# Three pairs of chunks as block products in the later FFNs, and weight splits of 2048 columns

## The chip, the cores and the metric

The kernel runs on one core of one Trainium2 chip. The metric is the device time of one execution in microseconds. The engines in the text are TensorE (PE, with its weight loads as PEld), VectorE (DVE), ScalarE (ACT), GpSimd (POOL) and SyncE (SP, which issues nearly all of the DMAs here).

## The reference

A streaming-encoder trunk of two layers on 256 tokens of width 1024, in float32. Each layer has three sub-layers, each between two RMS norms: an FFN, a mixer (differential attention beside an mLSTM), and a second FFN.

```python
def _swiglu(h, w_in, w_out):
    gate, up = jnp.split(h @ w_in, 2, axis=-1)
    return (jax.nn.silu(gate) * up) @ w_out
...
    for l in range(DEPTH):
        g = norm_gains[l]
        h = _swiglu(_rmsnorm(x, g[0]), ffn_w_in[l, 0], ffn_w_out[l, 0])
        x = x + 0.5 * _rmsnorm(h, g[1])
        lam_init = 0.8 - 0.6 * math.exp(-0.3 * l)
        h = _mixer(_rmsnorm(x, g[2]), mix_w_in[l], mix_w_out[l], da_lambda[l], da_subln_g[l],
                   lam_init, ml_conv_w[l], ml_conv_b[l], ml_gate_b[l], ml_norm_g[l])
        x = x + _rmsnorm(h, g[3])
        h = _swiglu(_rmsnorm(x, g[4]), ffn_w_in[l, 1], ffn_w_out[l, 1])
        x = x + 0.5 * _rmsnorm(h, g[5])
```

The hidden width of an FFN is 2816. w_in is 1024 x 5632 (gate and up), w_out 2816 x 1024.

## The kernel before

**Phases and chunks.** The six sub-layers are phases 0 to 5; phases 0, 2, 3 and 5 are FFNs. An FFN is cut into 11 chunks of 256 hidden columns. Tokens are two tiles of 128, t = 0 and 1. A chunk's in part multiplies the tokens with 512 columns of w_in (256 gate, 256 up). Its weights come as two pieces of 128 x 2048 floats, one for each half of the 1024 rows (kh = 0, 1). Its out part multiplies the hidden values with one piece of w_out and adds to four PSUM banks (bk), which collect over all of the chunks.

**Products in three matmuls.** Each float operand is split in a high part of reduced precision and the rest. A product is then three matmuls of 128 x 128 by 128 x 512: high by high, high by low, low by high (`mm3`, L506 to L508). A plain chunk's in part is 2 tokens x 8 row blocks x 3 = 48 matmuls, an out part 24.

**Splitting weights.** `fetch` (L288) loads a piece into a raw buffer (tag wr, three of them; every fourth piece goes to wx). `halved` (L295, L296) makes the high part with a cast on ScalarE and the low part with a subtraction on VectorE, 1024 columns at a time. The halves live in seven buffers each for wl and wh, and, for three halves out of ten, in two of the six k4 buffers: five pieces in all. In the mixer k4 holds that phase's own tiles (gt, conv, two qkT, vd), and no weights are put there. `self.turns` puts the first splits of a phase behind named operations of the norms around the phase's start.

**Pairs.** `pair(c)` does the in parts of chunks c and c+1 as one product of 2 x 2 blocks (token tiles by chunk columns) with seven block products P1 to P7 in place of eight (Strassen's scheme in Winograd's form). Each block product is 12 matmuls (L762). For it, `pair_blocks` makes four sums of weight pieces on VectorE (L322) and splits seven pieces in place of four: P1 is b11, P5 the sum b11 + b12, P6 that plus b22, P7 is b12 + b22, P2 is b21, P3 is b22, P4 the running sum plus b21. The running sum lies in two buffers, qk and wt (`spare`), which also hold the mixer's data, and in phases 2, 3 and 5 the normalised tokens of the phase. `pair_tokens` makes four sums of token blocks from these (L357 to L368, split at L676 and L677), in three steps S0, S1, S2. The results are put together by seven VectorE operations (u, v, h0; L780 to L799) and two silu.

**From hidden values to the out part.** The hidden values of a chunk must be turned before they can be multiplied with w_out: ScalarE sorts bytes into planes (L648), a DMA transposes (L650), ScalarE puts them together as hT (L656), then hh and hl are split off (L676, L677). There are four buffers each of hh and hl.

**Stationary weights.** The last chunk, 10, is done with the weights as the stationary operand (`in_turned`, L737 and L742), which gives the hidden values already turned, so that no DMA is needed. It wants each token's norm factor as a row (`token_scales`, L684) and its own evacuation (`ffn_block`, L695 to L700).

**Order.** `STEPS` is the order of an FFN after chunks 0 and 1: I is a plain chunk, P a pair, L the load of an out piece, O an out part, S a step of the token sums.

```python
STEPS = "I2 L1 S0 O0 I3 L2 S1 O1 S2 P4 L3 O2 L4 O3 I6 L5 O4 I7 L6 O5 P8 L7 O6 L8 O7 I10 L9".split()
END = (8, 9, 10)
```

The order of the instructions on each engine is set when the program is built, by the framework's planner: an instruction that stands earlier in the program (or under `high_priority`) goes first among those that the planner has as ready, and later ones pass it while it isn't. Buffers are given from the free ones in the same way. `after` adds an edge for the order alone. From "ending" to "running" TensorE follows program order: there the out parts of chunks 8 to 10 are done, first for token 0, then for token 1, with the norms and the next phase's first chunk between.

## Time and profile before

| | |
|---|---|
| median of 3 runs | 940.39 us (940.22 to 941.68) |
| the profiled execution | 940.3 us |
| its span, first to last instruction | 938.5 us |
| mean granted TensorE clock | 0.998 |
| HBM read | 177.01 MB, 190 GB/s over the span |

The page has the busy share of each engine; views by stage, by group and in order of time are behind it. The bounds of the phases are read from the transposes of the norms (L532): FFN 0 to 180, mixer to 288, FFN to 467, FFN to 643, mixer to 751, FFN to the end. In the views a name like `wl<-wr,wh` is the written tile and the read ones, `x12` is a count, `[0.80 <-PE ptr L532]` is idle time ahead of an instruction and what ended it. Matmuls are pipelined: one of 512 columns is listed with some 0.39 us, and the next starts 0.23 us after it.

### The profile page before, as it was taken

The page shows a single profiled execution, that of the slowest core. Times are in us where ns is not written, and L with a number is a line of the kernel's source. Part 1 is how long each engine was busy: PE and PEld are TensorE (multiplying, and loading weights), DVE is VectorE, ACT ScalarE, POOL GpSimd, SP SyncE. Part 2 cuts the span into 40 slices and gives each one's busy share as a digit, 9 for nine tenths or more (in the row PEclk, how much of TensorE's full clock was granted, in tenths as well). Part 3 has the DMA queues.
Part 4 walks back from the last instruction along what each step waited for, and adds up shares of the span by engine and source line. Part 5 has one row for each costly group of instructions (what it writes and reads, how often), then busy time and mean ns, then how long its engine had stood idle before and what let it go on. Part 6 is the DMA issues. An engine that isn't in the chain of part 4 may idle for free.

```text
span 938.5 us, 12082 instructions
## 1 busy us (share of the span) xinstructions
PE 931.4 (99%) x4427; PEld 771.5 (82%) x4427; DVE 775.5 (83%) x1079; ACT 668.4 (71%) x1033; POOL 29.4 (3%) x57
## 2 busy tenths in 40 slices
PE   9999999999999999999999999999999999999997
PEld 7888888888888888888888888888888888888885
DVE  7989797889867899788698987968898588986974
ACT  8967786677856868676587865866778478766862
POOL 2000000000020000000000000000001100000000
PEclk9999999999999999999999999999999999999999
DMA  9957857346362866838468585473554348486531
GB/s 354 342 169 275 251 192 218 119 152 221 138 232 90 303 167 225 303 107 309 121 237 257 172 267 189 155 237 135 189 193 169 146 157 302 148 300 184 186 115 46
DMA packets 69882, 189.34 MB, mean 202 GB/s; under 512 B 45274, under 2 KB 46426, under 8 KB 49086
## 3 DMA queue, kind: packets, MB, share of 16 engines
q1 hardware_dynamic: 69246, 187.95, 59.1%
q8 instruction: 35, 0.57, 0.2%
q10 hardware_dynamic: 576, 0.61, 0.2%
q14 instruction: 25, 0.20, 0.1%
HBM read 177.01 MB, written 1.05 MB: 190 GB/s over the span
## 4 chain that ended last, share of the span: by engine, by line
PE 99%; DVE 0%; ACT 0%; POOLq 0%; DVEq 0%; issue 0%; ACTq 0%
PE pin L506 11%; PE pin L508 10%; PE pin L507 10%; PE bk L506 10%; PE bk L507 10%; PE bk L508 10%; PE ptr L762 9%; PE pin L762 7%; PE ptr L507 3%; PE ptr L506 3%; PE ptr L508 3%; PE ptr L737 2%; PE pin L737 2%; PE ptr L532 1%; PE ptr L1100 1%; PE pin L742 1%
## 5 line engine op out<-in xcount | busy, mean ns | idle before, releaser
L296 DVE TENSOR_TENSOR wl<-wr,wh 128x1024 fp32r<-128x1024 f32 x262 | 313.6, 1221 | 42.2 <-ACT wh L295 39.4
L295 ACT ACTIVATE wh<-wr 128x1024 fp32r<-128x1024 f32 x262 | 269.5, 1055 | 55.9 <-PE bk L508 15.8
L506 PE MATMUL pin<-wh,both 128*128 128x512 f32 x432 | 171.3, 399 | 0.0
L507 PE MATMUL pin<-wl,both 128*128 128x512 f32 x432 | 168.4, 390 | 0.0
L508 PE MATMUL pin<-wh,both 128*128 128x512 f32 x432 | 168.2, 390 | 0.0
L507 PE MATMUL bk<-wl,hh 128*128 128x512 f32 x352 | 136.3, 389 | 0.0
L506 PE MATMUL bk<-wh,hh 128*128 128x512 f32 x352 | 135.8, 390 | 0.0
L508 PE MATMUL bk<-wh,hl 128*128 128x512 f32 x352 | 133.4, 389 | 0.0
L508 PEld LDWEIGHTS pin<-wh,both 128*128 128x128 f32 x432 | 81.1, 188 | 17.4
L506 PEld LDWEIGHTS pin<-wh,both 128*128 128x128 f32 x432 | 81.3, 188 | 17.2 <-issue 0.7
L507 PEld LDWEIGHTS pin<-wl,both 128*128 128x128 f32 x432 | 81.3, 188 | 15.5
L295 ACT ACTIVATE wh<-wx 128x1024 fp32r<-128x1024 f32 x62 | 64.3, 1055 | 31.9 <-PE bk L508 10.2
L762 PE MATMUL ptr<-wh,both 128*128 128x512 f32 x256 | 84.0, 389 | 0.0
L296 DVE TENSOR_TENSOR wl<-wx,wh 128x1024 fp32r<-128x1024 f32 x62 | 74.7, 1220 | 10.2 <-ACT wh L295 9.5
L508 PEld LDWEIGHTS bk<-wh,hl 128*128 128x128 f32 x352 | 66.1, 188 | 13.8
L506 PEld LDWEIGHTS bk<-wh,hh 128*128 128x128 f32 x352 | 66.1, 188 | 13.5
L507 PEld LDWEIGHTS bk<-wl,hh 128*128 128x128 f32 x352 | 66.1, 188 | 13.4
L762 PE MATMUL pin<-wh,both 128*128 128x512 f32 x192 | 63.0, 389 | 0.0
L762 PEld LDWEIGHTS ptr<-wh,both 128*128 128x128 f32 x256 | 48.0, 188 | 10.0
L507 PE MATMUL ptr<-wl,both 128*128 128x512 f32 x128 | 49.8, 389 | 0.0
L508 PE MATMUL ptr<-wh,both 128*128 128x512 f32 x128 | 49.8, 389 | 0.0
L762 PE MATMUL ptr<-wl,both 128*128 128x512 f32 x128 | 49.8, 389 | 0.0
(263 smaller groups left out, 1464.2 us busy)
## 6 DMA issues: line engine op xcount, KB each, us to landing
wr<-in_w_dram SPq DMA_DIRECT2D x131, 1024.0 KB, 5.1
wx<-in_w_dram SPq DMA_DIRECT2D x31, 1024.0 KB, 5.0
gpost<-in_gpost_dram SPq DMA_DIRECT2D x6, 512.0 KB, 6.2
wr<-in_w_dram SPq DMA_DIRECT2D x2, 512.0 KB, 6.3
wr<-in_w_dram SPq DMA_DIRECT2D x3, 256.0 KB, 4.5
x<-in_x_dram SPq DMA_DIRECT2D x3, 256.0 KB, 5.2
h<-planes SPq DMA_TRANSPOSE x32, 3.3
out_dram<-x SPq DMA_DIRECT2D x2, 256.0 KB, 2.1
```

The lines of the kernel that those rows point to most:

```text
L295: ia = nc.scalar.activation(hi, raw, AF.Copy)
L296: iv = nc.vector.tensor_tensor(lo, raw, hi.bitcast(F32), op=ALU.subtract)
L506: mm(ps, xh, wh, start=start, stop=False)
L507: mm(ps, xh, wl, start=False, stop=False)
L508: mm(ps, xl, wh, start=False, stop=stop)
L532: nc.tensor.transpose(ptr[:, k, :], x[:, (4 * hf + k) * P:(4 * hf + k + 1) * P], self.ident)
L737: self.nc.tensor.matmul(b, self.cols(w[kh], k)[0][:, c], both[kh][:, k].rearrange("p i t -> p (i t)"), start=kh == 0 and k == 0, stop=Fals ...
L742: self.nc.tensor.matmul(b[:, 0:NT * P], self.cols(w[kh], k)[1][:, c], both[kh][:, k, 0:NT].rearrange("p i t -> p (i t)"), start=False, sto ...
L762: self.nc.tensor.matmul(b, st[:, k, :], self.cols(w, k)[mv], start=new and k == n == 0, stop=k == 3 and n == 2, skip_group_check=True)
L1100: self.T(ptr[:, b, :], a[:, b * P:(b + 1) * P], self.tr.ident)
```

## The change

- **Two orders.** Phase 0 has `FIRST_STEPS` with the pairs (4,5) and (9,10) and plain chunks 6, 7 and 8. Phases 2, 3 and 5 have the new `STEPS` with three pairs, (2,3), (6,7) and (9,10), and plain chunks 4, 5 and 8. The token sums S0 to S2 now stand ahead of the pair (2,3) in these.
- **No stationary weights.** `in_turned`, `token_scales`, `ffn_block` and `ffn_turned` are gone. Chunk 10 is the second half of the last pair.
- **Wide splits.** A weight piece is cast and split in one operation of 2048 columns each (`whole`), and so are the block sums. In the mixer, and while `turns` has entries at a phase's start, pieces are split in halves as before.
- **Buffers.** wl and wh become one pool `w` of seven tiles of 2048 columns, and k4 has three such tiles. The mixer's k4 tiles are halves of one (`t4`). The running sum is one tile, `sums`; qk and wt are its halves.
- **Order on TensorE.** P4 of a pair is put behind the last matmul of P3. The second token of the out part of chunk 3 is put behind the pair (6,7), and that of chunk 6 and both of chunk 7 behind the pair (9,10).
- **Small moves.** The load of the post-norm gains and, in phase 0, of the mixer's constants is a step of its own, G0, behind O0. The first weight splits of the next phase are put behind the first token's operands of the last pair instead of those of chunk 10.

```diff
-STEPS = "I2 L1 S0 O0 I3 L2 S1 O1 S2 P4 L3 O2 L4 O3 I6 L5 O4 I7 L6 O5 P8 L7 O6 L8 O7 I10 L9".split()
+FIRST_STEPS = "I2 L1 S0 O0 G0 I3 L2 S1 O1 S2 P4 L3 O2 L4 O3 I6 L5 O4 I7 L6 O5 I8 L7 P9 L8 O6 L9".split()
+STEPS = "S0 S1 S2 P2 L1 O0 G0 I4 L2 O1 L3 O2 I5 L4 O3 P6 L5 O4 L6 O5 I8 L7 P9 L8 O6 L9".split()
...
     def t4(self, nm, shape):
-        return self.k4.tile(list(shape), F32, tag="k4", name=self.name(nm))
+
+        if self.lent is None:
+            pair = self.k4.tile([P, 2, 1024], F32, tag="k4", name=self.name(nm))
+            v, self.lent = pair[:, 0], pair[:, 1]
+        else:
+            v, self.lent = self.lent, None
+        return v[0:shape[0]].rearrange("p (a b) -> p a b", a=shape[1])
...
     def piece(self):
 
 
+        if self.four and not self.turns:
+            return self.whole(self.fetch())
         parts = self.begin_piece()
         return [parts(), parts()]
...
+    def whole(self, raw):
+
+        lo, hi = self.piece_tiles()
+        self.cut = self.nc.scalar.activation(hi, raw, AF.Copy)
+        self.nc.vector.tensor_tensor(lo, raw, hi.bitcast(F32), op=ALU.subtract)
+        return [(hi[:, j], lo[:, j]) for j in range(2)]
...
     def spare(self):
         if self.parts is None:
-            self.qk = self.ded.tile([P, 4, S], F32, name="qk")
-            self.wt = self.ded.tile([P, NT, 2, 2, P], F32, name="wt")
-            self.parts = [self.qk.rearrange("p b s -> p (b s)"), self.wt.rearrange("p t a b j -> p (t a b j)")]
+            self.sums = self.ded.tile([P, 2, 1024], F32, name="sums")
+            self.parts = [self.sums[:, j] for j in range(2)]
+            self.qk = self.parts[0].rearrange("p (b s) -> p b s", b=4)
+            self.wt = self.parts[1].rearrange("p (t a b j) -> p t a b j", t=NT, a=2, b=2)
         return self.parts
...
         def add(out, a, b):
-            for j in range(2):
-                self.nc.vector.tensor_tensor(out[j], a[j], b[j], op=ALU.add)
+            self.nc.vector.tensor_tensor(out, a, b, op=ALU.add)
...
+    def piece_tiles(self):
+
+        v = []
+        for nm in ("wl", "wh"):
+            pool, tag = (self.k4, "k4") if self.lend and self.tiles % 10 in (2, 5, 8) else (self.w, "w")
+            v.append(pool.tile([P, 2, 1024], F32R, tag=tag, name=self.name(nm)))
+            self.tiles += 1
+        return v
...
-        def out_part(c, t, h, wo):
+        def out_part(c, t, h, wo, behind=()):
             for hf in range(2):
                 for k in range(2):
-                    self.mm3(po[t][hf], *h[t][k], *self.cols(wo, 2 * k + hf),
-                             start=c == 0 and k == 0, stop=c == NC_FF - 1 and k == 1)
+                    i = self.mm3(po[t][hf], *h[t][k], *self.cols(wo, 2 * k + hf),
+                                 start=c == 0 and k == 0, stop=c == NC_FF - 1 and k == 1)
+                    self.after(i, behind)
...
-            product(b4, s4, w["P3"], False)
+            i = product(b4, s4, w["P3"], False)
...
-            product(b3, xT[1][1], w["P4"], False)
+            ended[c] = [product(b3, xT[1][1], w["P4"], False, [i])]
...
                 for t in range(NT):
-                    out_part(c, t, hs[c], wo[c])
-        rows = self.token_scales(r)
-        banks = [[self.bank_pin() for _ in range(2)], [self.bank_tr() for _ in range(2)]]
-        in_turned(banks, ws, both)
+                    out_part(c, t, hs[c], wo[c], ended.get(c + 3, []) if t else [])
+        wo[END[-1]] = self.piece()
+        pair_ready([self.cut])
 
         yield "ending"
-        with self.tc.high_priority():
-            hs[END[-1]] = self.ffn_turned(banks, rows)
-        wo[END[-1]] = self.piece()
+        for t in range(NT):
+            out_part(END[0] - 1, t, hs[END[0] - 1], wo[END[0] - 1], ended[END[0] + 1])
...
-        wr, wl, wh, trp, k4 = pool("wr", 3), pool("wl", 7), pool("wh", 7), pool("tr", 4), pool("k4", 6)
+        wr, w, trp, k4 = pool("wr", 3), pool("w", 7), pool("tr", 4), pool("k4", 3)
```

## The prediction

> **What bounds the kernel now.** I read the page's busy shares first, then the busy time by stage, the chain of waits, the groups of instructions by form, and last the order of time around a phase's start and around a pair.

> ```profile
> PE 931.4 (99%) x4427; PEld 771.5 (82%) x4427; DVE 775.5 (83%) x1079; ACT 668.4 (71%) x1033; POOL 29.4 (3%) x57
> ```
> ```profile
> 288.00:467.00 179.00, 179.00 (x815) 149.00 (x814) 149.86 (x184) 127.11 (x171) 2.18 (x4) 1.00 0.63 212
> 467.00:643.00 176.00, 176.00 (x800) 146.37 (x799) 148.24 (x183) 127.71 (x171) 2.32 (x6) 1.00 0.63 209
> ```

> The columns of the second fence are stretch, length, then busy time and count of PE, weight loads, DVE, ACT, POOL, granted clock, DMA share, GB/s. Each stretch is one FFN. TensorE is never idle in them, at full clock, so matmuls taken out are hidden by nothing. VectorE is the next engine: 148 to 150 us, 29 us below the stretch. The chain of waits, in order of time, shows the pitch of matmuls and what lies inside a pair:

> ```profile
> 426.00 1.13 PE pin L762 x5
> 427.13 0.23 PE bk L507
> 427.36 0.45 PE bk L508 x2
> ...
> 430.53 0.91 PE bk L506 x4
> 431.44 2.72 PE ptr L762 x12
> ```

> L762 is a block product: 12 matmuls in 2.72 us, 0.2267 each. The bk rows between are an out part (24 matmuls, 5.44 us): the pair's products leave holes, and out parts fill them. That cover decides this change.

> **What the change removes on TensorE.** A pair does the in part of two chunks in 7 x 12 = 84 matmuls, two plain chunks in 96. Phases 2, 3 and 5 get a third pair: 3 x 12 x 0.2267 = 8.2 us. Phase 0 keeps two pairs, at other chunks: 0. The stage with stationary weights (L737, L742, two transposes) goes in all four FFNs:

> ```profile
> 441.25 1.07 PE L737 MATMUL pin<-both,wh 128*128 128x512 f32 x4
> ```
> ```profile
> 452.63 0.40 PE L506 MATMUL bk<-wh,hh 128*128 128x512 f32 x1
> ```

> It runs from 441.25 to 452.63, 11.38 us, where a plain chunk costs 48 x 0.2267 = 10.88. So 0.50 goes four times, 2.0 us. Together TensorE loses 10.2 us of work. The profiled execution took 940.3 us (its span 938.5 and 1.8 around it, the median of the runs 940.39), so the floor is 930.1.

> **What it adds on VectorE and ScalarE.** The prices of the operations:

> ```profile
> L296 DVE TENSOR_TENSOR wl<-wr,wh 128x1024 fp32r<-128x1024 f32 x262 | 313.6, 1221 | 42.2 <-ACT wh L295 39.4 <-PE bk L508 1.5 <-ACT sil L267 0.8
> L677 DVE TENSOR_TENSOR hl<-hT,hh 128x256 fp32r<-128x256 f32 x80 | 31.2, 419 | 15.6 <-ACT hh L676 15.6
> L322 DVE TENSOR_TENSOR wt<-wt,wr 128x1024 f32<-128x1024 f32 x14 | 17.1, 1219 | 0.0
> L640 DVE SCALAR_TENSOR_TENSOR h<-pin,rs,sil 128x256 f32<-128x256 f32 x30 | 14.2, 478 | 2.6 <-ACT sil L267 2.6
> L697 DVE TENSOR_TENSOR su<-su,rows 128x256 f32<-128x256 f32 x16 | 6.6, 421 | 0.2
> L799 DVE SCALAR_TENSOR_TENSOR v<-v,rs,u 128x512 f32<-128x512 f32 x8 | 6.0, 745 | 0.0
> L784 DVE TENSOR_TENSOR v<-u,ptr 128x512 f32<-128x512 f32 x8 | 5.4, 681 | 0.0
> ```
> ```profile
> L295 ACT ACTIVATE wh<-wr 128x1024 fp32r<-128x1024 f32 x262 | 269.5, 1055 | 55.9 <-PE bk L508 15.8 <-PE ptr L762 12.3 <-PE pin L508 8.3
> L656 ACT ACTIVATE hT<-h 128x1024 uint16<-128x1024 uint16 x32 | 43.7, 1364 | 7.0 <-DMA h<-planes 7.0
> L648 ACT ACTIVATE planes<-h 128x1024 uint16<-128x1024 uint16 x32 | 33.6, 1050 | 17.5 <-DVE h L640 17.5
> L676 ACT ACTIVATE hh<-hT 128x256 fp32r<-128x256 f32 x80 | 29.0, 409 | 0.3
> L267 ACT ACTIVATE sil<-pin,rs 128x256 f32<-128x256 f32 x30 | 14.0, 466 | 16.1 <-PE pin L508 12.2 <-POOL rs L521 3.8
> L676 ACT ACTIVATE both<-aT 128x512 fp32r<-128x512 f32 x16 | 10.0, 624 | 1.8 <-DVE aT L365 1.7
> ```
> ```profile
> 353.86 3.50 DVE L296 TENSOR_TENSOR wl<-wr,wh 128x1024 fp32r<-128x1024 f32 x3
> ```

> No row has 2048 columns. From 512 to 1024 a DVE operation grows by 1.221 - 0.681 = 0.54, so I take 2.29 for 2048. Back to back, operations overlap: three in 3.50 is one each 1.14 us, 0.08 under the duration. So 2048 cost 2.21 where two halves cost 2.28: 0.07 saved a piece (bounds: 0, and 0.15 where neither form overlaps a neighbour). ScalarE: 1.055 + 2 x (1.055 - 0.624) = 1.92.

> [...]

> A third pair brings three more split pieces (3 x 2.21 = 6.6) and four more block sums (8.8). The 33 pieces and 8 sums that grow wide save 41 x 0.07 = 2.9. Evacuations nearly cancel: seven operations of 0.68 to 0.745 come, ten of about 0.42 from the turned stage go. VectorE goes from 149 to about 161.5 us per phase, TensorE from about 176 to 173: 93% instead of 84%. ScalarE gains three splits, 5.8, on 127, and follows. Loads stay at 33 pieces a phase. It fits on average, so each stretch must be looked at.

> **The new first pair, chunks 2 and 3.** Now it comes straight after chunks 0 and 1; before, two plain chunks stood there, in which VectorE gains on TensorE. The old clock of phase 3 shows the start:

> ```profile
> 475.96 1.29 DVE L539 TENSOR_TENSOR wt<-ptr,c 128x512 f32<-128x512 f32 x2 [0.80 <-PE ptr L532]
> ```
> ```profile
> 479.36 2.35 DVE L296 TENSOR_TENSOR wl<-wx,wh 128x1024 fp32r<-128x1024 f32 x2
> 481.63 2.35 DVE L296 TENSOR_TENSOR wl<-wr,wh 128x1024 fp32r<-128x1024 f32 x2
> ```
> ```profile
> 469.87 0.39 PE L506 MATMUL pin<-wh,both 128*128 128x512 f32 x1
> ...
> 475.32 1.03 PE L532 MATMUL ptr<-c,x 128*128 128x128 f32 x8
> 476.11 0.48 PE L506 MATMUL pin<-wh,both 128*128 128x512 f32 x1
> ```

> TensorE: chunks 0 and 1 are 96 matmuls, 21.8, and 0.8 of transposes from 469.87, so it wants P1 at 492.4. VectorE from 475.96: second prenorm 2.4, two pieces in halves 4.5, the token sums (eight 512 operations at 0.60 back to back) 4.8, three h 1.2, P1's split 2.2: 15.1, to 491.1. P1 is just in time. The first block sum may not start sooner: its buffer holds the normalised tokens that the sums read. Then sum to 493.3, ScalarE to 495.2 (VectorE meanwhile does the sum for P7), P5's split to 497.6. P1 ends on TensorE at 495.1, so P5 can come 2.5 late. Two things shorten this: the 0.80 idle ahead of 475.96, which P1's split may use, and the out part of chunk 0, whose operands come 2.7 (silu, hT, hh, hl) after chunk 1's last matmul, at about 495 to 497 if ScalarE isn't casting weights then. I take **1.8 us per phase**, bounds 0 and 2.5.

> From P5 on: five splits and two sums 15.5, evacuations before P4 3.1, hl 1.4, one out piece 2.2, together 22.2, to 519.8. TensorE from 497: five products 13.6 and the out parts of chunks 0 and 1, 10.9, to 521.5. With both out parts as cover P4 isn't late: I take 0. Without chunk 1's it is 3.7 late, without either 9.2. I take 0 because of the bk rows above.

> **The other two pairs.** From P6 to the end of P9, TensorE has two pairs 38.1, chunk 8 10.9, the out parts of 3, 4, 5 and half of 6 19.1: 68. VectorE: 20 pieces 44.2, eight sums 17.7, evacuations 9, hl and h 3.5, less what five buffers hold ready at P6 (three splits, two sums, 11): 63.4, or 93%. Around an old pair:

> ```profile
> 343.20:368.20 25.00, 24.22 (x27) 1.00 0.53 180
> ```

> It was busy 24.22 of 25 us there, 97%, with TensorE full. So I take 0; at 90% it would cost 2.4 a phase. Chunks 6 and 7 hold two of five buffers over P9 because half of their out parts is put behind it; three are left, each going round in about 7 us (cast 1.9, split 2.3, product 2.7), three products being 8.2. It suffices.

> The stationary stage needed no transpose by DMA; the last pair does, and this is the wait that the change adds:

> ```profile
> v<-planes SPq DMA_TRANSPOSE x8, 5.0
> ```

> From P4 to the operands of the second tokens of chunks 9 and 10 it is two DVE operations and a silu 2.1, planes 1.05, the transpose 5.0, hT 1.36, hh and hl 0.8: 10.3. Between lie half of chunk 6's out part, chunk 7's, and the first tokens of 8 to 10 and the second of 8: 84 matmuls, 19.0 us. Nothing is late, and no engine has work queued behind that wait which is wanted sooner. The load of the gains (gpost) moves behind the first pair; it is used at the phase's end only: 0.

> In the mixer the five k4 tiles come and go in pairs, and a weight buffer comes back a half piece later, 1.4 us, with three whole pieces in seven tiles, 16 us of matmuls against 4.2 for a split: 0, at most a few tenths a group.

> Sum: 930.1 + 3 x 1.8 = **935.5 us**.

> **Rivals.** (a) All covered: P5 arrives behind chunk 0's out part, 930.1 to 932. For it: TensorE had no hole in any FFN before. Against: VectorE is level with TensorE at P1, not ahead.

> (b) The waits give back what is gained: 8.4 to 12.2 us of waits, 2.8 to 4.1 a phase, gives 938.5 to 942.3, no change that can be told (0.2%, about 1.9 us). P5's full 2.5 and about 1 at P4 or P9 do that.

> (c) Slower: the cover fails in the first pair. Its place is P4 of chunks 2 and 3; the price is 3.7 us a phase without chunk 1's out part and 9.2 without either, beside P5's 2.5. It decides from 4 us a phase. With 6.2, the time is 930.1 + 18.6 = 948.7; with 11.7 it is 965. For it: chunk 1's out piece stands behind all seven splits in program order, and its h must be turned by DMA first. Against: the planner lets later work pass waiting work.

> (d) Long waits slow the clock. Matmuls after idle time:

> ```profile
> 5.49 0.78 PE L482 MATMUL bk<-wh,both 128*128 128x512 f32 x1
> 6.06 0.63 PE L483 MATMUL bk<-wh,both 128*128 128x512 f32 x1
> 6.49 0.54 PE L484 MATMUL bk<-wl,both 128*128 128x512 f32 x1
> ```
> ```profile
> 3.00:6.00 3.00, 3.00 (x14) 1.97 (x13) 1.06 (x3) 1.72 (x6) 0.97 (x4) 1.00 1.02 324
> ```

> They start 0.57 and 0.43 apart at the kernel's start, against 0.2267 later, though the granted clock of that stretch already reads 1.00; eight such would add 1.6 to 2.7 us per long wait. Over three phases that puts 5 to 8 us on top of (c), about 955. [...]

> **How the numbers follow.** Forecast 932 to 938.5: 0.37. (a) 0.18. (b) 0.20. (c) 0.19. (d) 0.06. Faster is (a) and the forecast, 0.55; same 0.20; slower 0.25. The range leaves out a little of (a) below and the worse half of (c) and (d): 930.5 to 949. The forecast's own is 932 to 938.5.

> **What would show it.** Right: TensorE 36 matmuls fewer in the three pairs, no L737; holes only in the first pair of phases 2, 3 and 5, between the first and second product, released by a split, 1 to 2.5 us each; VectorE at about 160 us a phase. Wrong: holes ahead of P4, in the mixer or ahead of chunk 10; out parts of chunks 0 and 1 behind the pair instead of in it; a 2048 split far from 2.29; a granted clock under 1.00 inside a phase.

## The result and the profile after

The kernel after takes 989.43 us (median of 4 runs, 988.95 to 990.38), the one before 940.31 beside it (939.9 to 941.68): 1.0521 times as long, 95% interval 1.0503 to 1.0539. The prediction was 935.5 us, with 930.5 to 949 as its range. It was wrong in size and in sign: 49 us slower, where 5 faster was forecast. One execution in the experiments below, of the run with three held pairs, was a slow one of 3324.77 us and is left out.

First the page of the kernel after, busy time and the groups of wide operations:

```profile
PE 941.0 (95%) x4319; PEld 764.1 (77%) x4319; DVE 804.8 (82%) x902; ACT 672.8 (68%) x884; POOL 29.0 (3%) x57
...
L317 DVE TENSOR_TENSOR wl<-wr,wh 128x2048 fp32r<-128x2048 f32 x83 | 189.4, 2286 | 27.5 <-issue 13.9
L316 ACT ACTIVATE wh<-wr 128x2048 fp32r<-128x2048 f32 x83 | 158.0, 1910 | 61.6 <-PE ptr L738 31.7
```

TensorE has 108 instructions fewer, as the change says, and yet its busy time grew from 931.4 to 941.0: some matmuls ran slowly. The durations of the 2048 forms, 2.286 and 1.910, are those the prediction estimated (2.29 and 1.92).

Then busy time by stage (stretch, length, busy time and count of PE, weight loads, DVE, ACT, POOL, granted clock, DMA share, GB/s); phase 0, a mixer, phases 2 and 5:

```profile
0.00:187.50 187.50, 180.93 (x787) 144.69 (x788) 148.08 (x151) 131.15 (x152) 7.02 (x22) 1.00 0.73 236
187.50:297.10 109.60, 107.60 (x593) 88.75 (x592) 86.19 (x165) 76.03 (x164) 7.37 (x10) 1.00 0.47 168
297.10:490.20 193.10, 183.15 (x786) 148.85 (x785) 162.80 (x143) 130.84 (x136) 2.17 (x4) 0.97 0.60 198
...
785.70:987.20 201.50, 183.84 (x796) 148.99 (x794) 161.66 (x146) 128.85 (x136) 2.72 (x5) 0.98 0.51 168
```

TensorE, which was never idle in these stages, now is in all of them. Phase 0, which kept two pairs, is 7.6 us longer than before (same boundaries, the first transposes of each phase); phase 2 is 14.0 longer, phase 3 9.5, phase 5 with the end 13.3, each mixer 2.1. VectorE has its 161 to 163 us in phases 2 and 5, as reckoned; the average was right and did not decide.

The view of waits for TensorE (us in all, times, longest) names what ended last:

```profile
PE ptr L738 <- DVE v L763: 8.5, 3, 3.8
PE ptr L738 <- ACT wh L316: 5.2, 4, 1.3
PE ptr L738 <- DVE wl L317: 5.0, 3, 2.1
...
PE bk L1195 <- DVE md L1185: 4.0, 2, 2.0
PE pin L530 <- DVE h L665: 2.9, 3, 1.2
```

All the waits of this view come to 39.2 us; before they were 0.8. To see what a hole costs altogether, I added up, over the order of time of TensorE, what each step from one matmul's start to the next takes above its usual pitch (0.2267 for 512 columns). That gives 58.7 us after and 2.7 before. Of the 58.7, 28.8 lie at the last pair (5.0, 9.0, 5.1 and 9.6 in the four phases), 20.2 at the first pair of phases 2, 3 and 5 (7.6, 6.6, 6.0), 5.6 in the mixers, 4.1 elsewhere, most of it in phase 0 and at the kernel's start. The pair at chunks 6 and 7 has none. 56.0 came; less the 10.2 us of removed work that is 45.8. The spans differ by 48.7, so 2.9 are left unexplained.

The difference between the two sums, 19.5 (1.9 of it was there before), lies in the steps around a wait. Some 9.5 us of it are matmuls that run at half clock for a while. Some 7 come with each wait anew, about 0.27: at 332.60 the step from the matmul before is 0.16 longer than pitch and idle time together, and the step to the next, at 332.94, 0.11 longer than the pitch. In phase 2 after, in order of time on TensorE (start, length, instruction, in brackets the idle time before it and what ended it):

```profile
332.60 0.50 PE L738 MATMUL ptr<-wl,both 128*128 128x512 f32 x1 [2.09 <-DVE wl L317]
...
352.62 0.79 PE L531 MATMUL bk<-wl,hh 128*128 128x512 f32 x1 [1.60 <-DVE wl L306]
353.21 0.63 PE L532 MATMUL bk<-wh,hl 128*128 128x512 f32 x1
353.64 0.63 PE L530 MATMUL bk<-wh,hh 128*128 128x512 f32 x1
...
355.77 0.49 PE L532 MATMUL bk<-wh,hl 128*128 128x512 f32 x1
356.10 0.40 PE L530 MATMUL bk<-wh,hh 128*128 128x512 f32 x1
...
447.37 0.49 PE L738 MATMUL ptr<-wh,both 128*128 128x512 f32 x1 [1.29 <-ACT wh L316]
...
461.14 0.47 PE L738 MATMUL ptr<-wh,both 128*128 128x512 f32 x1 [3.61 <-DVE v L763]
```

After an idle time of 1.60 matmuls start 0.43 apart until 355.77, twice the usual pitch, then 0.23 again. The same comes after the 1.29 at 447.37 and, from 462.00 on, after the 3.61 at 461.14, but not after the 2.09 at 332.60. The last section shows what decides.

The longest wait, at 461.14, is P3 of the last pair: it adds on the bank in which P5 was computed, and v's second evacuation (L763) still has to read it. VectorE in that stretch:

```profile
440.98 2.29 DVE L334 TENSOR_TENSOR sums<-sums,wr 128x2048 f32<-128x2048 f32 x1
445.56 2.29 DVE L317 TENSOR_TENSOR wl<-sums,wh 128x2048 fp32r<-128x2048 f32 x1 [2.29 <-ACT wh L316]
...
457.17 0.68 DVE L762 TENSOR_TENSOR v<-u,ptr 128x512 f32<-128x512 f32 x1
457.77 2.29 DVE L317 TENSOR_TENSOR wl<-sums,wh 128x2048 fp32r<-128x2048 f32 x1
459.97 0.42 DVE L702 TENSOR_TENSOR hl<-hT,hh 128x256 fp32r<-128x256 f32 x1
460.31 0.68 DVE L763 TENSOR_TENSOR v<-v,ptr 128x512 f32<-128x512 f32 x1
460.91 2.29 DVE L317 TENSOR_TENSOR wl<-wr,wh 128x2048 fp32r<-128x2048 f32 x1
465.75 0.69 DVE L769 TENSOR_TENSOR h<-ptr,u 128x512 f32<-128x512 f32 x1 [2.55 <-PE ptr L738]
```

A sum ends at 443.27, ScalarE's cast of it runs from 443.62 to 445.53, the split can't start before; meanwhile VectorE stands idle for 2.29, with nothing else in hand. From 445.56 to 463.2 it is never idle. The evacuation that TensorE waits for could start when L762 ends, at 457.85. It starts at 460.31, behind hl and a split of a sum, which at this point is the block of P4, wanted one product later: 2.5 of the 3.61 us are order in VectorE's queue.

### The profile page after: what moved, and what is told of

Read it like the earlier page. It is cut to its first block, busy times and chain, and to the rows that moved or that the text cites. A ratio compares the mean times of both kernels' runs of the same rounds, so it can differ in the third digit from the quotient of the medians.

```text
span 987.2 us, 11529 instructions
## 1 busy us (share of the span) xinstructions
PE 941.0 (95%) x4319; PEld 764.1 (77%) x4319; DVE 804.8 (82%) x902; ACT 672.8 (68%) x884; POOL 29.0 (3%) x57
## 3 DMA queue, kind: packets, MB, share of 16 engines
HBM read 177.01 MB, written 1.05 MB: 180 GB/s over the span
## 4 chain that ended last, share of the span: by engine, by line
PE 65%; DVE 12%; issue 5%; ACT 2%; DVEq 0%; POOLq 0%; ACTq 0%
PE bk L531 8%; PE ptr L738 8%; PE bk L532 8%; PE bk L530 8%; PE pin L530 7%; PE pin L532 7%; PE pin L531 7%; DVE wl L317 4%; PE pin L738 3%; DVE wl L306 2%; DVE sums L334 2%; ACT wh L316 1%; PE ptr L532 1%; PE ptr L531 1%; PE ptr L530 1%
## 5 line engine op out<-in xcount | busy, mean ns | idle before, releaser
L317 DVE TENSOR_TENSOR wl<-wr,wh 128x2048 fp32r<-128x2048 f32 x83 | 189.4, 2286 | 27.5 <-issue 13.9
L316 ACT ACTIVATE wh<-wr 128x2048 fp32r<-128x2048 f32 x83 | 158.0, 1910 | 61.6 <-PE ptr L738 31.7
L530 PE MATMUL pin<-wh,both 128*128 128x512 f32 x448 | 178.1, 400 | 3.3 <-DVE h L665 2.9
L532 PE MATMUL pin<-wh,both 128*128 128x512 f32 x448 | 174.8, 390 | 0.0
L532 PE MATMUL bk<-wh,hl 128*128 128x512 f32 x352 | 132.6, 391 | 0.0
L738 PE MATMUL ptr<-wh,both 128*128 128x512 f32 x352 | 117.8, 401 | 13.7 <-DVE v L763 8.5
L306 DVE TENSOR_TENSOR wl<-wr,wh 128x1024 fp32r<-128x1024 f32 x96 | 114.2, 1220 | 14.2 <-ACT wh L305 12.3
L305 ACT ACTIVATE wh<-wr 128x1024 fp32r<-128x1024 f32 x96 | 96.6, 1050 | 14.7 <-PE bk L532 6.7
L317 DVE TENSOR_TENSOR wl<-sums,wh 128x2048 fp32r<-128x2048 f32 x33 | 75.5, 2287 | 28.3 <-ACT wh L316 26.3
L532 PEld LDWEIGHTS pin<-wh,both 128*128 128x128 f32 x448 | 84.1, 188 | 18.1
L738 PEld LDWEIGHTS ptr<-wh,both 128*128 128x128 f32 x352 | 68.3, 194 | 30.5 <-issue 9.7
L738 PE MATMUL pin<-wh,both 128*128 128x512 f32 x264 | 87.2, 396 | 0.0
L316 ACT ACTIVATE wh<-sums 128x2048 fp32r<-128x2048 f32 x33 | 63.2, 1914 | 26.7 <-PE pin L738 11.7
L532 PEld LDWEIGHTS bk<-wh,hl 128*128 128x128 f32 x352 | 66.5, 189 | 13.9 <-DVE hl L702 0.2
L738 PE MATMUL ptr<-wl,both 128*128 128x512 f32 x176 | 70.9, 403 | 5.0 <-DVE wl L317 5.0
```

The source lines that it names most:

```text
L305: ia = nc.scalar.activation(hi, raw, AF.Copy)
L306: iv = nc.vector.tensor_tensor(lo, raw, hi.bitcast(F32), op=ALU.subtract)
L316: self.cut = self.nc.scalar.activation(hi, raw, AF.Copy)
L317: self.nc.vector.tensor_tensor(lo, raw, hi.bitcast(F32), op=ALU.subtract)
L530: first = mm(ps, xh, wh, start=start, stop=False)
L532: mm(ps, xl, wh, start=False, stop=stop)
```

## The experiments

The question at the start was whether the width of operations and buffers makes the new waits, or the new order of pairs, plain chunks and out parts; then what in the order. Each expectation states the theories, and the letters, that it sets against each other. Times are single runs unless a range or an interval stands with them; the kernel before took 940.0 to 941.0 beside each of them. Of each edit the lines that matter are shown, and of an order only the part that differs.

**Operations of 1024 in the new buffers.**

```diff
-        self.cut = self.nc.scalar.activation(hi, raw, AF.Copy)
-        self.nc.vector.tensor_tensor(lo, raw, hi.bitcast(F32), op=ALU.subtract)
+        for j in range(2):
+            self.cut = self.nc.scalar.activation(hi[:, j], raw[:, j], AF.Copy)
+            self.nc.vector.tensor_tensor(lo[:, j], raw[:, j], hi[:, j].bitcast(F32), op=ALU.subtract)
...
-            self.nc.vector.tensor_tensor(out, a, b, op=ALU.add)
+            for j in range(2):
+                self.nc.vector.tensor_tensor(out[:, j], a[:, j], b[:, j], op=ALU.add)
```

> The changed kernel with its buffers, orders and three pairs, but every split and block sum in two operations of 1024 columns again. Theory W (wide operations): the chain sum, cast, split of a pair (2.2 + 1.9 + 2.2 us) runs one after the other with 2048 columns and overlaps with 1024, so TensorE's waits in the pairs of all four FFNs shrink: 950 to 965 us. Theory B (buffers held): the waits in the last pair come from chunks 6 and 7 keeping two of five buffers, width does not matter: 980 to 992. Theory V (VectorE short of time): a piece costs 0.07 us more in halves, so it gets slower: 990 to 1000.

984.22 us, in B's band. The wait for v is still there, 15.6 us in four waits. Halving the operations gives back 5 us of 49.

**Out parts set free.** The edges that hold chunk 7's out part and half of chunk 6's behind the last pair are taken out. Chunk 3's out part never had one, other than the section on the change says: O3 stands ahead of P6 in the order, so `ended` has no entry for that pair yet.

```diff
-                    out_part(c, t, hs[c], wo[c], ended.get(c + 3, []) if t else [])
+                    out_part(c, t, hs[c], wo[c], [])
...
-            out_part(END[0] - 1, t, hs[END[0] - 1], wo[END[0] - 1], ended[END[0] + 1])
+            out_part(END[0] - 1, t, hs[END[0] - 1], wo[END[0] - 1])
```

> The changed kernel without the edges that put the out parts of chunks 3, 6 and 7 behind a pair; they may fill holes in the pair and give their buffers back early. Theory B: the last pair's waits go in all four FFNs (about 5 us in phase 0, 5 to 9 in the others): 960 to 968 us. Theory W: the chain stays as slow, out parts fill only part of it: 975 to 985. Theory V: no change, 985 to 992.

1009.75 us, outside of every band. The waits went to the phase's end: 33.8 us in five waits for hh, the longest 9.5. The out parts are wanted in two places, inside the pair and behind it.

**Two pairs in all phases**, phase 0's order everywhere, wide operations kept.

```diff
-        steps = STEPS if kept else FIRST_STEPS
+        steps = FIRST_STEPS
```

> The changed kernel with the order of phase 0 (pairs 4,5 and 9,10) in all four FFNs. Theory V: two pairs ask for no more of VectorE than before, so it is back at 938 to 945 us. Theories W and B: every phase is like phase 0, which took 7.6 us more than before; with mixers 2 us longer each that is 940 + 4 x 7.6 + 4 = 970 to 978.

977.92 us, at the upper end of the band of W and B: without any third pair 38 of the 49 us are still there, where the last pair alone has moved and the operations are wide.

**Wide alone.** The kernel before, in its own order, with the new buffers, splits and sums.

```diff
-        def split(raw):
-            return [self.halved(raw[j]) for j in range(2)]
+        fetch, split = self.fetch, self.whole
...
-            for j in range(2):
-                self.nc.vector.tensor_tensor(out[j], a[j], b[j], op=ALU.add)
+            self.nc.vector.tensor_tensor(out, a, b, op=ALU.add)
...
-        wr, wl, wh, trp, k4 = pool("wr", 3), pool("wl", 7), pool("wh", 7), pool("tr", 4), pool("k4", 6)
+        wr, w, trp, k4 = pool("wr", 3), pool("w", 7), pool("tr", 4), pool("k4", 3)
```

> The kernel before (old orders, two pairs, stationary weights, no edges on out parts) with only the wide splits, wide sums and buffers of 2048 columns. Theory W: the two pairs of each FFN have longer chains, and the waits appear: 955 to 970 us. Theories B and V: nothing is held longer and VectorE has less work: 938 to 944.

957.73 us, in W's band: in the order of before width costs 17.7. ScalarE of this run in phase 2, at the pair's end:

```profile
451.24 1.92 ACT L315 ACTIVATE wh<-wx 128x2048 fp32r<-128x2048 f32 x1 [5.79 <-PE ptr L785]
453.06 0.70 ACT L274 ACTIVATE u<-u,rs 128x512 f32<-128x512 f32 x1
...
455.48 1.04 ACT L671 ACTIVATE planes<-h 128x1024 uint16<-128x1024 uint16 x1
...
462.76 1.34 ACT L679 ACTIVATE hT<-h 128x1024 uint16<-128x1024 uint16 x1 [2.49 <-DMA h<-planes]
```

A cast of a whole piece stands at the head of the queue for 5.79 us, until a product gives a whole buffer back. The silu and the planes that the last operands need stand behind it, and TensorE waits for hh at 464.99 (7.3 us in three waits in all).

**The new buffers with operations of 1024, in the order of before.** To the run above comes the edit of the first run:

```diff
+        for j in range(2):
+            self.cut = self.nc.scalar.activation(hi[:, j], raw[:, j], AF.Copy)
+            self.nc.vector.tensor_tensor(lo[:, j], raw[:, j], hi[:, j].bitcast(F32), op=ALU.subtract)
```

> The kernel before with buffers of 2048 columns, and splits and sums still in two operations of 1024. Theory C: the buffers alone cost, so about what the wide form took: 952 to 962 us. Theory W (wide operations): the width costs, so it goes back to 939 to 944.

943.85 us, in W's band. So 14 of the 17.7 are the operations and 3 the buffers. Of these 2.0 is one wait in a mixer for md, the same that the kernel after has in both mixers (4.0 us in two waits).

**The kernel after on small buffers and operations**, without the edges in a second run.

```diff
-        fetch, split = self.fetch, self.whole
...
+        def split(raw):
+            return [self.halved(raw[j]) for j in range(2)]
...
-        wr, w, trp, k4 = pool("wr", 3), pool("w", 7), pool("tr", 4), pool("k4", 3)
+        wr, wl, wh, trp, k4 = pool("wr", 3), pool("wl", 7), pool("wh", 7), pool("tr", 4), pool("k4", 6)
```

> The changed kernel, three pairs with its orders and edges, on the buffers, splits and sums of the kernel before (tiles of 1024 columns). Theory C (coarse buffers): a buffer of 2048 columns comes back only when all of it is used, casts wait for it at the head of ScalarE's queue and hold up the steps behind them; with small buffers most of the waits go: 930 to 945 us. Theory O (orders): the pair behind chunk 8 and the early pair are what VectorE can't serve, whatever the buffers: 960 to 975.

> As the run with small buffers, and without the edges that put out parts behind a pair. Theory C: the edges only guard the time that the last pair's hidden values need for their transposes, as seen with large buffers (22 us lost without them), so some 10 to 20 us more than with them: 945 to 960 us. Theory O: the out parts fill the holes of the pairs: less than with the edges by 5 or more.

988.42 and, without the edges, 985.13 us (where 16.6 us of waits for hh stand behind the pairs in place of those for v). C falls, and O's bands are missed too: the first run is slower than O said, and without the edges it gains 3.3, not 5. (With the large buffers the edges were worth 20.3 us, 1009.75 against 989.43, where the expectation has 22.) The new order, with buffers and operations as before, costs 47 us, nearly all of the loss. The waits have other names (15.8 for v, 6.8 for ACT wh, 5.0 for wl), the same places and the same sum (57.3 us above the usual pitch; 58.7 in the kernel after). The width that costs 17.7 in the old order costs 1 to 2 in the new one, no more than single runs scatter; I read it so that it lengthens chains that are late anyway.

**Two pairs, small buffers**: the edit above and phase 0's order everywhere. From before differ the last pair's place, the missing stage, the small moves and P4 behind P3; O7 and half of O6 are held behind the pair. All but the place and the held out parts stays in a later run that takes 940.30 us. Against the kernel before:

```diff
-I6 L5 O4 I7 L6 O5 P8 L7 O6 L8 O7 I10 L9
+I6 L5 O4 I7 L6 O5 I8 L7 P9 L8 O6 L9
```

> The order of phase 0 (pairs 4,5 and 9,10, no stationary weights) in all four FFNs on the small buffers of the kernel before. TensorE has 2.0 us less work than before. Theory C: 938 to 943 us. Theory O: the last pair right behind chunk 8 still waits: 955 to 970.

972.21 us, a little over O's band. With the number of products unchanged, the last pair's move, with what it does to the out parts, costs 31 us, 7.8 a phase. Waits of TensorE, and two stretches of phase 2:

```profile
PE pin L715 <- DVE wl L297: 10.9, 6, 3.5
PE ptr L715 <- DVE v L740: 7.6, 3, 3.5
```
```profile
405.00:430.00 25.00, 25.00 (x113) 20.68 (x111) 17.91 (x18) 12.48 (x15) 0.00 (x0) 1.00 0.68 201
...
450.00:462.00 12.00, 8.49 (x28) 6.47 (x27) 7.96 (x10) 4.35 (x6) 0.00 (x0) 0.72 0.48 175
```

While the three plain chunks 6, 7 and 8 run, VectorE is busy 17.91 of 25 us: it could work ahead and mostly has no free buffer. Its longest idle times there, 2.77 and 2.63, end with a cast that itself waited for a matmul to give a buffer back:

```profile
408.89 1.06 ACT L296 ACTIVATE wh<-wr 128x1024 fp32r<-128x1024 f32 x1 [2.98 <-PE ptr L509]
...
409.99 2.59 DVE L297 TENSOR_TENSOR wl<-wr,wh 128x1024 fp32r<-128x1024 f32 x2 [2.63 <-ACT wh L296]
```

Two shorter ones, 1.31 and 1.26, end with a load. Then VectorE is the engine that the pair waits for.

**The first pair alone.** The kernel before, with the pair of chunks 4 and 5 moved to 2 and 3 in phases 2, 3 and 5; the number of products stays.

```diff
-I2 L1 S0 O0 I3 L2 S1 O1 S2 P4 L3 O2 L4 O3 I6 L5 O4 I7
+S0 S1 S2 P2 L1 O0 G0 I4 L2 O1 L3 O2 I5 L4 O3 I6 L5 O4 I7
```

> The kernel before, its buffers, splits, end with stationary weights and last pair (8,9), with the first pair of phases 2, 3 and 5 moved from chunks 4 and 5 to 2 and 3, right behind chunks 0 and 1. TensorE has the same work as before. Theory E (the early pair costs by its place: VectorE is level with TensorE there and can't serve a pair): about 8 us in each of three phases, 958 to 968 us. Theory H (only the last pair, behind chunk 8 with out parts held behind it, costs): 939 to 946.

960.43 us, in E's band: 19.6 more, 6.5 in each of three phases. The first rows of its view of waits:

```profile
PE ptr L763 <- DVE wl L297: 4.8, 6, 1.0
PE bk L508 <- DVE wl L297: 3.9, 2, 2.0
PE pin L507 <- DVE h L641: 1.9, 3, 0.6
PE ptr L763 <- DVE v L787: 1.9, 1, 1.9
```

Many small waits: ahead of the pair (h), at P5 (the first row: 0.6 and 1.0 at its two halves in each phase), later in the pair (v) and at the out parts' operands.

**Both out parts ahead of the last pair**, in the run with two pairs, without edges.

```diff
-I8 L7 P9 L8 O6 L9
+I8 L7 O6 O7 P9 L8 L9
```

> As the run with two pairs on small buffers (972 us), with the out parts of chunks 6 and 7 ahead of the last pair instead of behind it. Theory H: the last pair waits because the weights of chunks 6 and 7 hold two of five buffers and nothing fills its holes; with all five buffers the waits in it (about 8 us a phase) go, and the transposes of the last pair's hidden values now show at the end, some 4 us a phase: 955 to 966 us. Theory D (VectorE cannot do a pair behind a single plain chunk, however many buffers): the waits in the pair stay and those at the end come on top: 975 to 990.

969.87 us, between the bands of H and D. No wait is left in the pair; instead

```profile
PE bk L507 <- ACT hh L678: 20.6, 4, 5.3
```

one in each phase, for the last operands, which nothing covers now. I read this as held buffers in the pair or bare transposes behind it, one or the other. If so, one out part ahead and one behind should serve both.

**One ahead, one behind**: chunk 7's stays held behind the pair.

```diff
-I8 L7 P9 L8 O6 L9
+I8 L7 O6 P9 L8 L9
```

> The run with two pairs on small buffers (972.2), with one out part (chunk 6) put ahead of the last pair and the other (chunk 7) left behind it. If the 31 us of that run are the held buffers and the cover together (theory H), one freed buffer lets VectorE run ahead and 5.4 us of out part still cover the last transposes: both waits go, 939 to 950. If VectorE is simply behind at the pair, whatever buffers it has (theory S), the waits inside the pair stay: 962 to 972.

972.91 us: theory H falls, and S comes within 1 us of its band. TensorE waits 24.7 us in four waits, all for v. Phase 2, two lines of the run before and then two of this one:

```profile
454.05 0.39 PE L507 MATMUL bk<-wh,hh 128*128 128x512 f32 x1
454.41 0.68 DVE L740 TENSOR_TENSOR v<-v,ptr 128x512 f32<-128x512 f32 x1
...
454.08 0.68 DVE L740 TENSOR_TENSOR v<-v,ptr 128x512 f32<-128x512 f32 x1
454.81 0.80 PE L715 MATMUL ptr<-wh,both 128*128 128x512 f32 x1 [5.49 <-DVE v L740]
```

VectorE comes to v at nearly the same time in both, and at 453.43 in the run that gives no buffer back early, though that run's phase 0 ended 1.4 to 2.0 us later. So buffers given back early don't make it faster. What differs is how TensorE fills the wait: with both out parts ahead 36 of their 48 matmuls run between the products of the pair, 12 of them from 454.05 on; here chunk 6's 24 all run before the pair and its 84 products follow one another with nothing between. So one out part inside the pair and one behind it is not what ran, and stays untested.

**The end of before, with a plain chunk 10.** The last pair is back at 8 and 9; chunk 10 follows without stationary weights, in all phases; chunk 7's out part comes last, held by nothing.

```diff
-I8 L7 P9 L8 O6 L9
+P8 L7 O6 L8 I10 L9
```

> The last pair stays at chunks 8 and 9 as before, in the order of before, and chunk 10 comes last as a plain chunk with its transpose by DMA, covered by chunk 7's out part and two halves of 8 and 9 (10.9 us); the stage with stationary weights is gone in all four phases, nothing else is changed. If the place of the last pair is what costs (theory H), this keeps the whole gain of the missing stage, 4 x 0.5: 937 to 941. If the stage hides more than its half microsecond, a cover of the last chain that nothing else gives (theory T), the waits come back at the end: 948 to 965.

954.15 us (951.62 to 955.66), ratio 1.0146, 1.0129 to 1.0163: in T's band, with waits for hh at the end. ScalarE in phase 2 shows the bare chain:

```profile
459.27 1.06 ACT L650 ACTIVATE planes<-h 128x1024 uint16<-128x1024 uint16 x1 [1.04 <-DVE h L642]
464.39 1.34 ACT L658 ACTIVATE hT<-h 128x1024 uint16<-128x1024 uint16 x1 [4.06 <-DMA h<-planes]
465.76 0.72 ACT L678 ACTIVATE hh<-hT 128x256 fp32r<-128x256 f32 x2
```

Chunk 10's last matmul starts at 456.08, its operands come at 466.2: 9.9 us, of which the transpose takes 4. The planner had put half of chunk 7's out part ahead of chunk 10, so only 27 matmuls, 6.1 us, stood against it, and TensorE waited 3.64.

**The same with chunk 7's out part held behind chunk 10.**

```diff
-                        in_piece(t, kh, pins[t], ws[kh])
+                        last = in_piece(t, kh, pins[t], ws[kh])
...
-            out_part(END[0] - 1, t, hs[END[0] - 1], wo[END[0] - 1])
+            out_part(END[0] - 1, t, hs[END[0] - 1], wo[END[0] - 1], [last])
```

> The run with a plain end (954.2), with chunk 7's out part tied behind chunk 10's last in matmul. There the planner had put the first half of that out part into chunk 10's place, so that 6.1 us of matmuls stood against a chain of 9.9 from chunk 10's last matmul to its operands, and TensorE waited 1.1 to 3.6. With it held, 10.9 stand against 9.9. If the missing cover is all that the plain end costs (theory E), the waits and the slow matmuls behind them go: 937 to 942, which may be 0.2% faster than before. If that half was needed as filler at the pair (theory F), the wait goes to the pair's products or the first matmuls of chunk 10: 945 to 955.

940.30 us (938.87 to 942.42, 12 runs) against 940.69, ratio 0.9997, 0.9989 to 1.0005. Theory E: the waits are gone, and so falls T, since the stage gives no cover that a held out part doesn't. Phase 2 of this run, with TensorE busy throughout at full clock:

```profile
287.00:466.00 179.00, 179.00 (x800) 148.36 (x799) 148.01 (x174) 128.17 (x167) 2.17 (x4) 1.00 0.64 213
```

So the last pair's 31 us go with its place: at 9, three ways to put the out parts of 6 and 7 around it cost 29 to 32, at 8 it costs nothing. How I read it: a plain chunk behind the pair covers the pair's operands with its own 48 matmuls, so that the out parts of 5 and 6 can fill the pair, and chunk 7's covers the end.

**A third pair between the two**, at 6 and 7 in phases 2, 3 and 5, in the kernel of the last run; first and last pair keep their places.

```diff
-P4 L3 O2 L4 O3 I6 L5 O4 I7 L6 O5 P8
+P4 L3 O2 L4 O3 P6 L5 O4 L6 O5 P8
```

> The same with a third pair at chunks 6 and 7 in phases 2, 3 and 5, between the old two, which keep their places at 4 and 8; on buffers and operations of 1024 columns. If only the places of the first and last pair cost (theory H), the third pair's 36 missing matmuls pay in full: 8.2 under the run with two pairs and a held out part, 929 to 935 where that gives 937 to 942. If VectorE at some 93% cannot feed three pairs in a row (theory V), waits come at the second and third pair: 945 to 965.

979.83 us (978.97 to 982.65, 3 runs), ratio 1.0411, 1.0393 to 1.0429: H falls, and the waits cost more than V said. Stretch of phase 2 that holds the second and third pair:

```profile
380.00:440.00 60.00, 51.68 (x211) 39.86 (x210) 59.17 (x64) 45.05 (x54) 0.00 (x0) 0.97 0.56 190
```

VectorE is busy 59.17 of 60 us, TensorE 51.68. Here VectorE has nothing to spare for 60 us on end. That it alone is the bound is not shown: 19.9 of the 34.9 us of waits end on hh of ScalarE, and from 418.36 to 423.11 five casts run ahead of planes whose v was ready at 418.62.

**Three pairs at other places.** Two runs in the kernel before, with its end, in phases 2, 3 and 5 (pairs at 3, 6, 8 and at 3, 5, 8); and the second order with a plain chunk 10 whose cover was not held, which, other than its expectation says, has the three pairs in phase 0 too.

```diff
+I2 L1 S0 O0 G0 S1 S2 P3 L2 O1 L3 O2 I5 L4 O3 P6 L5 O4 L6 O5 P8 L7 O6 L8 O7 I10 L9
...
+I2 L1 S0 O0 G0 S1 S2 P3 L2 O1 L3 O2 P5 L4 O3 L5 O4 I7 L6 O5 P8 L7 O6 L8 O7 I10 L9
...
+I2 L1 S0 O0 G0 S1 S2 P3 L2 O1 L3 O2 P5 L4 O3 L5 O4 I7 L6 O5 P8 L7 O6 L8 I10 L9
```

> The kernel before with its buffers and its end with stationary weights, and three pairs (3,4), (6,7), (8,9) in phases 2, 3 and 5: TensorE's floor is 940.3 - 8.2 = 932. Theory E/H (each pair needs VectorE ahead by plain chunks in front of it): the first pair is covered by chunk 2, the last follows another pair and waits some 5 to 10 us a phase: 948 to 965 us. Theory C2 (the end without transposes is what counts): 933 to 940.

> As the run with pairs at 3, 6 and 8, with the pairs at (3,4), (5,6) and (8,9): two pairs in a row early, a plain chunk ahead of the last one. Theory E/H: the second pair of the row waits 5 to 10 us a phase, the last one is covered by chunk 7 as before: 945 to 960 us. Theory C2: 933 to 940.

> Three pairs at chunks 3, 5 and 8 in phases 2, 3 and 5, none directly behind chunks 0 and 1 and none at the end, chunk 10 plain with chunk 7's out part as cover; phase 0 as in the run with a plain end. The same pairs with the old end gave 974.9, with 19.5 us waits on the last operands and slow matmuls after them. If places and the end are all that costs (theory H), 935 to 950. If VectorE at 93% can't feed three pairs wherever they stand (theory V), 958 to 975.

978.64, 974.91 and 1016.66 us, each above all bands of its expectation. The largest waits in all three are for hh, operands of out parts: 15.7, 19.5 and 44.1 us. In the second run they stand right behind the pair at 5 (5.3 and 4.0 in phase 2), not at the end where the third run's expectation put them, so the third run, which has the bare end besides (6.20 ahead of 497.32), can't tell H from V. What they share with the other runs of three pairs is the result: no place tried for a third pair gave less than 34 us over the kernel before.

## Why the prediction was wrong, point by point

- **The arithmetic of the floor** held as far as the trace counts: 108 matmuls fewer, L737 gone, and where nothing waits the pitch is 0.2267. The 2.0 us for the stage with stationary weights are not confirmed: the run with a held out part 7, which has little else of the change, lies between 1.0 less and 0.5 more than before by its interval.
- **Prices of operations** held (2.29 and 1.91, 161 to 163 us of VectorE in a phase), and the step "It fits on average, so each stretch must be looked at" was right. The later stretches were then looked at with sums over 25 to 70 us, and that is what failed.
- **The first pair, 1.8 per phase, bounds 0 and 2.5**, was 6.7 (20.2 in three), and 6.5 where nothing else was changed (960.43). The lateness of P5 was seen rightly, 2.09 at 332.60. What was missed comes before and after: h waits 1.2 ahead of the pair, and "With both out parts as cover P4 isn't late: I take 0" fails, since the out parts' own operands are late (the wait for wl at 352.62). They go through the same VectorE that the pair has made late. Cover that must first be made ready by the late engine is no cover. Rival (c) was nearer for this pair: its 3.7 beside 2.5 make 6.2 a phase, and its mechanism, chunk 1's out piece behind the splits, is part of what is seen.
- **The last pair, "It suffices"**, is the costliest failure: 0 forecast, 28.8 measured, 31 alone. The step compared VectorE and TensorE over 68 us and gave three buffers a turn of 7 us against 8.2. Three things stood against it in the runs. VectorE can't use its lead time, because its buffers are mostly full while chunks 6 to 8 run (17.91 of 25 busy, with two pairs). A sum, its cast and its split are one after the other on two engines, 6.9 us from 440.98 to 447.85, and VectorE idled 2.29 within. And evacuations stand in order behind splits: of the 3.61 that P3 waited, 2.5 were that. Another order in this queue was not tried, so how much of the 31 us it would give back at the same place is open.
- **The transposes covered, 10.3 against 19.0**, was right for the kernel after: no wait for the last operands. But the cover was chunk 7's out part and half of chunk 6's, held behind the pair, and the prediction didn't ask what the pair loses by it. Put ahead, they end the waits in the pair and bare the end (969.87); and where chunk 6's ran before the pair, chunk 7's alone behind it left the pair bare (972.91).
- **The pair at 6 and 7: 0** was right in the kernel after: it has no wait. It is not free by itself, as the run with three held pairs shows, where it comes right between two others.
- **The mixer, "0, at most a few tenths a group"**, was 2.0 of wait each, from the new buffers (each mixer is 2.1 longer; the run with new buffers and 1024 operations has the wait, the one with small buffers not). In the mixer of the kernel after, VectorE does a rotation and a split ahead of md, where before only the split stood.
- **The width, 0.07 saved a piece**, was right as a price and wrong as an effect. In the kernel after wide splits in a row start 2.20 apart (343.47 and 345.68 in phase 2: 2.21), against the 2.28 of two halves, so it is 0.07. In the order of before the width costs 17.7, of which 14 go with the operations; the cast that blocks ScalarE's queue is one stretch of it.
- **Rival (d), the slow clock**, had a chance of 0.06; what came on top of the waits is some 18 of the 56.0 us, half clock 9.5 of these. The eight slow matmuls after a wait were an estimate, since the rows of the start show three; in the kernel after, a period at half clock holds 8 (352.54 to 355.95 in the last section), 1.6 us more than at full, the lower end of the rival's 1.6 to 2.7. The doubled pitch, 0.43, goes with the granted clock there, 0.50. The length of a single wait does not tell: 1.60 was enough at 352.62, and 2.09 twenty us earlier was not. What decided in the traces is how much idle time falls into one period of the clock: 1.95 us or more was followed by half clock in 60 cases of 60 (last section).

None of the rivals priced the mechanism that cost most, the last pair, whose price comes in all four phases, phase 0 too, where the prediction expected no change.

## What to carry to other kernels

Independent work that fills holes is a budget: write down for each piece which hole it fills, and what the other holes then lack; here the out parts held to cover what follows a pair were missing in the pair. A share of 93% over a phase says nothing about a stretch where the same engine has to make the cover ready as well, and a lead counts only as far as there are buffers to hold it. Put the construct with bare ends (a block product, a long chain to its operands) between plain work on both sides, and leave operations as long as the most urgent one behind them in the queue can wait.

## What the runs showed of the hardware

Twice the pitch of matmuls (0.43 against 0.2267) follows idle times as short as 1.3 to 1.6 us. What comes on top of the waits is some half of them again (58.7 against 39.2 in the kernel after, 34.3 against 20.6 with two pairs, where 2.7 against 0.8 is the kernel before); in the kernel after about half of that is half clock. The granted clock shows it only over short stretches: 0.72 over the 12 us shown for two pairs, 0.98 over the whole of that phase.

```profile
328.65:332.06 3.41, 1.86 (x9) 1.19 (x7) 3.41 (x3) 2.91 (x4) 0.00 (x0) 1.00 0.93 376
332.06:335.47 3.41, 2.87 (x13) 2.38 (x14) 3.38 (x4) 2.40 (x4) 0.00 (x0) 1.00 0.54 136
349.13:352.54 3.41, 1.76 (x6) 0.67 (x4) 3.41 (x5) 1.33 (x2) 0.00 (x0) 1.00 0.97 396
352.54:355.95 3.41, 3.33 (x8) 2.65 (x9) 3.41 (x4) 1.91 (x1) 0.00 (x0) 0.50 0.42 106
458.36:461.77 3.41, 0.63 (x3) 0.58 (x4) 3.41 (x4) 1.69 (x1) 0.00 (x0) 1.00 0.84 329
461.77:465.18 3.41, 3.41 (x10) 2.66 (x9) 1.42 (x1) 0.00 (x0) 0.00 (x0) 0.50 0.27 50
```

A period with much idle time is followed by one at half clock. I summed TensorE's idle time by period over the 19 traces: after 1.95 us or more the next period was at half in 60 cases of 60, after less than 1.3 in none of some 5000, between the two in 11 of 43 (the kernel's start and end left out). So the 2.09 ahead of 332.60, which a bound at 332.06 cuts in two, did nothing, and several short waits in one period add up: in the run with two pairs in all phases and wide operations, after waits of 1.77 and 1.30 that end at 931.04 and 932.84, matmuls are 0.43 apart from 933.93 on. In the run with the first pair alone, 15.2 us of waits brought no half clock before the kernel's end.
